# A two-block transformer kernel: the first up-projection of the second feed-forward scaled between the normed chunks, and products of zeros in the waits at the begin

## The chip, the cores and the metric

The kernel runs on one core of a Trainium2 chip. The metric is device time in microseconds: the median of several runs of the whole kernel, one launch each. TensorE is called PE here, VectorE DVE, ScalarE ACT, GpSimd POOL, and SyncE SP; SP issues most of the DMAs.

## The reference, cut to what matters

Two blocks of two layers each work on 256 tokens of width 1024 (first block: differential attention, then neighbourhood attention, each followed by a convolutional feed-forward, with a second stream of 256 context tokens; second block: two hybrid layers). The change touches the begin of the first layer and the feed-forward of the second layer:

```python
def rmsnorm(t, g):
    tf = t.astype(jnp.float32)
    tf = tf * lax.rsqrt(jnp.mean(tf * tf, axis=-1, keepdims=True) + NORM_EPS)
    return tf.astype(t.dtype) * g

def conv_ffn(t, w_up, w_conv, b_conv, w_down):
    n = t.shape[1]
    u = t @ w_up
    half = CONV_W // 2
    up = jnp.pad(u, ((0, 0), (half, half), (0, 0)))
    acc = b_conv
    for tap in range(CONV_W):
        acc = acc + up[:, tap:tap + n] * w_conv[tap]
    a, g = jnp.split(acc, 2, axis=-1)
    return (jax.nn.silu(g) * a) @ w_down
...
    for i in range(DEPTH):
        sh1, sc1, g1, sh2, sc2, g2 = jnp.split((silu_c @ ada_w[i] + ada_b[i])[:, None, :], 6, axis=-1)
        h = rmsnorm(x, norm_mix[i]) * (1.0 + sc1) + sh1
        ...
        x = x + g1 * y
        h2 = rmsnorm(x, norm_ffn[i]) * (1.0 + sc2) + sh2
        x = x + g2 * conv_ffn(h2, ffn_up[i], ffn_conv[i], ffn_conv_b[i], ffn_down[i])
```

## The kernel before

**Data and products.** Activations stand transposed, model dimension on the partitions: `xT` is 8 chunks (kc) of 128 rows by 512 columns, 256 tokens of x and 256 of the context. Every fp32 product is made of three products of shorter floats: an operand is split into a high and a low part, and `mm3` (L332, L335, L336) adds hi·hi, hi·lo and lo·hi in PSUM. `whi` and `wlo` are the parts of a weight tile: ACT copies `whi` from `raw` (L311), DVE subtracts to get `wlo` (L312). A normed chunk is made by three instructions: DVE's `nt` (L544: x times the column A times the token's factor `nbc`), ACT's `hhi` (L545), DVE's `hlo` (L546). A weight tile holds two units of 1024 columns, so it costs two L311 and two L312.

**Norms.** A norm sums squares (`naccx`, `naccc`), takes the mean over the partitions on PE (L512), computes the factor `nrstd` on POOL, spreads it over the partitions on PE (L532), and ACT copies it to `nbc` (L537). The modulation (`ada`) is a matrix-vector product: L384 on PE, ACT's copy `apart` (L393), L399 on PE, and three small DVE instructions that give the columns A and B.

**The begin.** `layer0` loads x, the first modulation piece and weights, calls `warm(14)`, which multiplies a tile of zeros by itself 14 times into an S bank, then makes the first norm, the modulation of chunk 0, the normed chunks 0 and 1 and their part of the V projection (L780). That stretch is in an order written by hand for PE, ACT and DVE; everything else is ordered by the Tile scheduler, which simulates the engines and lists each engine's instructions once. At run time each engine takes its list strictly in that order.

**PSUM.** Banks come from three pools: `acc` (2), `S` (3), `misc` (3). `acc5` takes acc and S in turn.

**The feed-forward.** Each up-projection j makes two tiles (`which` 0 and 1: the value and the gate) of 128 rows by 256 tokens over 8 chunks, 24 products each. Of the second layer's 22 up-projections, the first three are made before the norm is known, from x·A (`up_z`, `up_z_late`): their PSUM tiles (`pre[0]`, `pre[1]`, `pre[2]`; in `ffn` the list is `pre` and its pair of tiles `pz`) hold 256 unscaled columns and two columns of the shift. Once `nbc` is there, DVE copies the shift (L618, tag `nvar`, two buffers, the same tag as a small tile of `norm_rstd`), multiplies the tile by `nbc` into an `nt` buffer (L619), and ACT adds the shift (L620). After that come the convolution's three taps (ACT L625, DVE L628, POOL; for later up-projections DVE L628 and L637 read the PSUM tile itself), silu (L642) and the product on POOL.

**The chain.** `chain` (L719) plans two groups of norm steps that are set between the products of the late up-projections, 14 and 8 products apart: the mean, then the broadcast and the normed chunks. In the second layer all eight chunks are emitted there; then `up_z` of `pre[2]` goes out, and `ffn` begins, with the scalings of `pre[0]` first.

## Time and profile before

| | us |
|---|---|
| median of 3 runs | 1577.13 (1576.31 to 1577.66) |
| the profiled execution | 1575.77 |
| its span in the trace | 1574.0 |
| PE busy in the span | 1543.0 |
| DVE busy | 1118.6 |
| ACT busy | 770.7 |
| mean granted PE clock | 0.996 of full |

All rows below are of one execution. A window row gives the busy time of each engine and the granted clock of that stretch; a timeline row gives the start, the time from the first instruction's start to the last one's end, the instruction, its tiles and in brackets the idle time before it with what ended it. Consecutive instructions of a kind are one row, and neighbours overlap a little, so that start to start is a little shorter than one duration.

### The profile page before, as it was taken

To read this page: it belongs to the slowest core of one execution; us is meant where nothing else is said; L and a number is where in the kernel's file an instruction comes from. 1 tells how busy PE (TensorE), PEld (TensorE's weight loads), DVE (VectorE), ACT (ScalarE), POOL (GpSimd) and SP (SyncE) were. 2 spreads that over 40 slices of the span, in tenths; PEclk is the share of its full clock that TensorE was granted. 3 is DMA by queue.
4 is the path that set the end of the run, shared out by engine and by line. 5 is a ranking of instruction groups with operands and counts; after the bars stand their busy time and mean duration, and the time that the engine had idled before them with its cause. 6 is when DMAs were issued, how large, how long until landed. Compare 5 with 4: busy or idle time off the path is not lost.

```text
span 1574.0 us, 26745 instructions
## 1 busy us (share of the span) xinstructions
PE 1543.0 (98%) x10426; PEld 1352.5 (86%) x10426; DVE 1118.6 (71%) x2010; ACT 770.7 (49%) x1387; POOL 349.6 (22%) x419
## 2 busy tenths in 40 slices
PE   8999999999999999999999999999999999999998
PEld 6777777888888888888777999999899999989998
DVE  5456767787999999463554786777767667867665
ACT  4445544554422344343454574665655445555443
POOL 0012211321100111210112150124435123352222
PEclk9999999999999999999999999999999999999999
DMA  8523333134557554234221345547435556425552
GB/s 345 185 81 134 119 150 122 61 141 166 184 198 276 193 204 149 89 107 149 106 108 68 139 167 191 192 152 257 153 111 183 194 201 215 160 97 198 172 205 82
DMA packets 49373, 251.93 MB, mean 160 GB/s; under 512 B 5088, under 2 KB 8160, under 8 KB 31584
## 3 DMA queue, kind: packets, MB, share of 16 engines
q1 hardware_dynamic: 49248, 250.23, 44.3%
q8 instruction: 82, 1.34, 0.3%
q14 instruction: 43, 0.35, 0.1%
HBM read 249.16 MB, written 1.05 MB: 159 GB/s over the span
## 4 chain that ended last, share of the span: by engine, by line
PE 88%; DVE 5%; DMA 2%; ACT 2%; issue 1%; POOL 1%; SPq 0%; POOLq 0%; DVEq 0%; ACTq 0%
PE acc L332 13%; PE acc L336 13%; PE acc L335 12%; PE S L332 10%; PE S L336 10%; PE S L335 10%; PE S L1116 3%; PE S L780 2%; DMA raw<-in_aqk 1%; PE misc L1058 1%; PE misc L1165 1%; PE misc L1053 1%; PE misc L335 1%; PE misc L332 1%; PE misc L336 1%
## 5 line engine op out<-in xcount | busy, mean ns | idle before, releaser
L311 ACT ACTIVATE whi<-raw 128x1024 fp32r<-128x1024 f32 (+2 forms) x372 | 372.1, 1007 | 428.2 <-PE acc L335 167.9
L312 DVE TENSOR_TENSOR wlo<-raw,whi 128x1024 fp32r<-128x1024 f32 (+2 forms) x372 | 439.3, 1185 | 173.8 <-ACT whi L311 172.5
L332 PE MATMUL acc<-hhi,whi 128*128 128x256 f32 (+1 forms) x800 | 264.4, 331 | 2.0 <-DVE nt L619 1.4
L336 PE MATMUL acc<-hhi,wlo 128*128 128x256 f32 (+1 forms) x800 | 262.5, 329 | 0.3 <-DVE wlo L312 0.3
L335 PE MATMUL acc<-hlo,whi 128*128 128x256 f32 (+1 forms) x800 | 261.7, 327 | 0.1
L332 PE MATMUL S<-hhi,whi 128*128 128x256 f32 (+1 forms) x584 | 187.0, 320 | 1.8 <-DVE u L637 1.8
L336 PE MATMUL S<-hhi,wlo 128*128 128x256 f32 (+1 forms) x584 | 186.1, 319 | 0.0
L335 PE MATMUL S<-hlo,whi 128*128 128x256 f32 (+1 forms) x584 | 185.5, 318 | 0.0
L332 PEld LDWEIGHTS acc<-hhi,whi 128*128 128x128 f32 x800 | 150.3, 188 | 20.7 <-issue 6.3
L336 PEld LDWEIGHTS acc<-hhi,wlo 128*128 128x128 f32 x800 | 150.2, 188 | 17.7 <-issue 4.0
L335 PEld LDWEIGHTS acc<-hlo,whi 128*128 128x128 f32 x800 | 150.1, 188 | 16.4 <-issue 3.8
L441 DVE SCALAR_TENSOR_TENSOR junk<-araw,cb 128x1024 bf16<-128x1024 f32 x112 | 146.1, 1304 | 3.6 <-ACT cb L429 3.2
L643 POOL TENSOR_TENSOR u<-u,u 128x256 f32<-128x256 f32 (+1 forms) x46 | 58.2, 1266 | 371.7 <-ACT u L642 371.6
L332 PEld LDWEIGHTS S<-hhi,whi 128*128 128x128 f32 x584 | 111.4, 191 | 9.2 <-ACT ghi L361 2.0
L336 PEld LDWEIGHTS S<-hhi,wlo 128*128 128x128 f32 x584 | 111.1, 190 | 8.4
L335 PEld LDWEIGHTS S<-hlo,whi 128*128 128x128 f32 x584 | 111.1, 190 | 8.0
L1500 POOL TENSOR_TENSOR macc<-macc,mm 128x256 f32<-128x256 f32 x48 | 48.4, 1008 | 163.4 <-DVE mm L1498 163.4
L332 PE MATMUL acc<-hlo,whi 128*128 128x256 f32 x288 | 82.1, 285 | 0.0
L336 PE MATMUL acc<-hlo,wlo 128*128 128x256 f32 x288 | 81.5, 283 | 0.0
L335 PE MATMUL acc<-hhi,whi 128*128 128x256 f32 x288 | 81.4, 283 | 0.0
L332 PE MATMUL S<-ghi,whi 128*128 128x256 f32 (+1 forms) x209 | 68.6, 328 | 0.0
L336 PE MATMUL S<-ghi,wlo 128*128 128x256 f32 (+1 forms) x209 | 68.3, 327 | 0.0
(437 smaller groups left out, 3617.9 us busy)
## 6 DMA issues: line engine op xcount, KB each, us to landing
raw<-in_up SPq DMA_DIRECT2D x44, 1024.0 KB, 4.9
raw<-in_mg SPq DMA_DIRECT2D x32, 1024.0 KB, 5.2
araw<-in_adav SPq DMA_DIRECT2D x56, 512.0 KB, 4.2
raw<-in_t SPq DMA_DIRECT2D x24, 1024.0 KB, 4.8
raw<-in_down SPq DMA_DIRECT2D x32, 704.0 KB, 4.1
raw<-in_ada SPq DMA_DIRECT2D x16, 1024.0 KB, 4.9
raw<-in_aqk SPq DMA_DIRECT2D x8, 1024.0 KB, 5.9
raw<-in_bqk SPq DMA_DIRECT2D x8, 1024.0 KB, 4.9
```

Source lines behind the costliest of these rows:

```text
L311: nc.scalar.activation(hi[:, :n], raw, AF.Copy)
L312: nc.vector.tensor_tensor(lo[:, :n], raw, hi[:, :n].bitcast(F32), op=ALU.subtract)
L332: first = nc.tensor.matmul(ps, wh, x[0], start=start, stop=False)
L335: nc.tensor.matmul(ps, wh, x[1], start=False, stop=False)
L336: nc.tensor.matmul(ps, wl, x[0], start=False, stop=stop)
L441: nc.vector.scalar_tensor_tensor(junk, self.araw, 1.0, self.acb[0][:, c, :], op0=ALU.mult, op1=ALU.mult, accum_out=self.ada[l][:, v, k, c ...
L643: nc.gpsimd.tensor_tensor(us[0], us[0], us[1], op=ALU.mult)
L780: nc.tensor.matmul(ps, (hhi, hlo)[a][:, kc, c], w[b][:, f], start=(kc == 0 and e == 0), stop=(kc == KC - 1 and e == 2))
L1053: nc.tensor.transpose(tp[:, t * P : t * P + P], p[:, t * P : t * P + P], self.ident)
L1058: nc.tensor.matmul(o[64 * j : 64 * j + 64, :], v[:, t, (2 * h + j) * 64 : (2 * h + j) * 64 + 64], pT[:, j, t, :], start=(t == 0), stop=(t ...
L1116: m = self.nc.tensor.matmul(sps[j][:, :n], q[a][r, qs], k[b][r, ks], start=(e == 0), stop=(e == 2))
L1500: nc.gpsimd.tensor_tensor(acc, acc, m, op=ALU.add)
```

## The change

Three edits. The zero tile is made once and its products go to a `misc` bank instead of an S bank; there are 18 in front, and 2, 1 and 3 in three later places of the hand-written order. The scaling of an up-projection's tile moves into a helper `pz_scale`, and its shift gets a tag of its own, `pzs`. In the second layer, `chain` emits only chunks 0 to 3; then the two tiles of `pre[0]` are scaled, and then the chunks 4 to 7 are normed.

```diff
...
     def warm(self, n):
-        z = self.t(self.nrm, [P, T], "nbc", bufs=3)
-        self.nc.gpsimd.memset(z, 0.0)
-        ps = self.sb()
+        if self.zero is None:
+            self.zero = self.t(self.nrm, [P, T], "nbc", bufs=3)
+            self.nc.gpsimd.memset(self.zero, 0.0)
+        ps = self.misc()
         for _ in range(n):
-            self.nc.tensor.matmul(ps[:, 0:T], z[:, 0:P], z, start=True, stop=True)
+            self.nc.tensor.matmul(ps[:, 0:T], self.zero[:, 0:P], self.zero, start=True, stop=True)
+
+    zero = None
...
+    def pz_scale(self, pz, bc):
+
+        ps = self.t(self.nrm, [P, T], "nt", bufs=5)
+        shift = self.t(self.nrm, [P, 2], "pzs", bufs=2)
+        self.nc.vector.tensor_copy(shift, pz[:, T : T + 2])
+        self.nc.vector.tensor_tensor(ps, pz[:, 0:T], bc, op=ALU.mult)
+        return ps, shift
...
                         if pz:
-                            ps = self.t(self.nrm, [P, T], "nt", bufs=5)
-                            shift = self.t(self.nrm, [P, 2], "nvar", bufs=2)
-                            nc.vector.tensor_copy(shift, pz[which][:, T : T + 2])
-                            nc.vector.tensor_tensor(ps, pz[which][:, 0:T], bc, op=ALU.mult)
+                            ps, shift = pz[which] if isinstance(pz[which], tuple) else self.pz_scale(pz[which], bc)
                             nc.scalar.activation(ps, ps, AF.Identity, bias=shift[:, 0:1])
...
-    def chain(self, n, l, w, h, st, hh, done=None):
+    def chain(self, n, l, w, h, st, hh, done=None, kcs=range(KC)):
...
-            for kc in range(KC):
+            for kc in kcs:
...
-            self.warm(14)
+            self.warm(18)
...
                 rstd = self.norm_rstd(sts[0])
+                self.warm(2)
                 parts = self.ada_parts(0, ada[0])
+                self.warm(1)
                 bcs[0] = self.norm_bcast(rstd)
                 self.ada_columns(0, *parts)
+                self.warm(3)
...
-            self.chain((14, 8), 1, 1, 0, st2, (hhi, hlo), done)
+            self.chain((14, 8), 1, 1, 0, st2, (hhi, hlo), done, range(4))
             pre = self.up_z_late(1, range(2), 2)
             pre.append(self.up_z(1, 2, (self.misc, self.misc)))
             self.flush()
             bc = done[0]
+            pre[0] = pre[0][0], [self.pz_scale(ps, bc) for ps in pre[0][1]]
+            for kc in range(4, KC):
+                self.norm_half(1, 1, 0, kc, hhi, hlo, bc)
```

What this makes of the engines' lists is shown at three places. Rows read: line, operation, written tile, read tiles, and a count for equal rows; in the changed kernel the lines of `split`, `mm3` and the norm stand 3 lower down (L312 is L315, L544 is L547), those of `ffn` and `layer0` 8 lower down (L628 is L636, L780 is L788), and L605 and L606 of `pz_scale` do what L618 and L619 did. First PE at the kernel's begin, before (`nbc` is the tile of zeros in its first row, L512 the mean, L384 and L399 the modulation, L532 the broadcast, L780 the V projection):

```order
L303 MATMUL S_106<-nbc_104 128x256 x14
L512 MATMUL misc_143<-cst_69,p_132 128x2 x4
L384 MATMUL misc_152<-raw_95,cs_73 32x256 x8
L532 MATMUL misc_163<-cst_69,nrstd_150 128x128 x2
L399 MATMUL misc_152<-cst_69,apart_161 128x128 x2
L384 MATMUL misc_182<-ohi_88,cs_73 32x256 x8
L780 MATMUL acc_124<-whi_174,hhi_121 128x512
L780 MATMUL acc_125<-whi_174,hhi_121 128x512
```

And the same with the change:

```order
L304 MATMUL misc_106<-nbc_104 128x256 x18
L515 MATMUL misc_147<-cst_69,p_136 128x2 x4
L304 MATMUL misc_156<-nbc_104 128x256 x2
L387 MATMUL misc_159<-raw_95,cs_73 32x256 x8
L304 MATMUL misc_170<-nbc_104 128x256
L535 MATMUL misc_172<-cst_69,nrstd_154 128x128 x2
L402 MATMUL misc_159<-cst_69,apart_168 128x128 x2
L304 MATMUL misc_183<-nbc_104 128x256 x3
L387 MATMUL misc_195<-ohi_88,cs_73 32x256 x8
L788 MATMUL acc_128<-whi_187,hhi_125 128x512
L788 MATMUL acc_129<-whi_187,hhi_125 128x512
```

The zero products write misc tiles now and stand in four places, each ahead of a step that waits for another engine or a DMA.

Next ACT in the V projection of layer 0, where its last chunks are normed (`apart` is the modulation's copy); before:

```order
L311 ACTIVATE whi_103_543<-raw_98_511 128x1024
L311 ACTIVATE whi_114_595<-raw_113_593 128x1024
L393 ACTIVATE apart_95_493<-misc_94_484 128x256
L311 ACTIVATE whi_116_599<-raw_113_593 128x1024
L545 ACTIVATE hhi_18_121<-nt_101_517,ada0_6_76 128x256
L545 ACTIVATE hhi_18_121<-nt_102_533,ada0_6_76 128x256
L545 ACTIVATE hhi_18_121<-nt_105_547,ada0_6_76 128x256
L545 ACTIVATE hhi_18_121<-nt_106_563,ada0_6_76 128x256
```

With the change:

```order
L314 ACTIVATE whi_106_556<-raw_101_524 128x1024
L314 ACTIVATE whi_117_608<-raw_116_606 128x1024
L548 ACTIVATE hhi_18_125<-nt_104_530,ada0_6_76 128x256
L396 ACTIVATE apart_98_506<-misc_97_497 128x256
L548 ACTIVATE hhi_18_125<-nt_105_546,ada0_6_76 128x256
L314 ACTIVATE whi_119_612<-raw_116_606 128x1024
L548 ACTIVATE hhi_18_125<-nt_108_560,ada0_6_76 128x256
L548 ACTIVATE hhi_18_125<-nt_109_576,ada0_6_76 128x256
```

Two of the four hhi that stood behind the second whi of that weight tile (`whi_116`, now `whi_119`) now stand ahead of it, one of them ahead of `apart` too.

Last DVE ahead of the second layer's feed-forward, before (`acc_1455` and `S_1456` are the two tiles of `pre[0]`; `nt_1473` to `nt_1476` are the chunks 4 to 7, and the last of the L546 in a row is chunk 4's):

```order
L312 TENSOR_TENSOR wlo_1514_8169<-raw_1510_8162,whi_1513_8168 128x1024
L546 SCALAR_TENSOR_TENSOR hlo_1449_7853<-nt_1470_7960,ada1_7_77,hhi_1448_7852 128x256
L546 SCALAR_TENSOR_TENSOR hlo_1449_7853<-nt_1471_7964,ada1_7_77,hhi_1448_7852 128x256
L546 SCALAR_TENSOR_TENSOR hlo_1449_7853<-nt_1472_7968,ada1_7_77,hhi_1448_7852 128x256
L546 SCALAR_TENSOR_TENSOR hlo_1449_7853<-nt_1473_7972,ada1_7_77,hhi_1448_7852 128x256
L544 SCALAR_TENSOR_TENSOR nt_1474_7976<-xT_3_71,nA11_11_81,nbc_1468_7954 128x256
L312 TENSOR_TENSOR wlo_1521_8237<-raw_1519_8234,whi_1520_8236 128x1024
L544 SCALAR_TENSOR_TENSOR nt_1475_7980<-xT_3_71,nA11_11_81,nbc_1468_7954 128x256
L544 SCALAR_TENSOR_TENSOR nt_1476_7984<-xT_3_71,nA11_11_81,nbc_1468_7954 128x256
L619 TENSOR_TENSOR nt_1486_8084<-acc_1455_7864,nbc_1468_7954 128x256
L312 TENSOR_TENSOR wlo_1523_8241<-raw_1519_8234,whi_1522_8240 128x1024
L619 TENSOR_TENSOR nt_1490_8095<-S_1456_7865,nbc_1468_7954 128x256
```

With the change, from the first of chunk 0 to 3 on (the tiles of `pre[0]` are `acc_1458` and `S_1459`):

```order
L547 SCALAR_TENSOR_TENSOR nt_1472_7969<-xT_3_71,nA11_11_81,nbc_1471_7967 128x256
L547 SCALAR_TENSOR_TENSOR nt_1473_7973<-xT_3_71,nA11_11_81,nbc_1471_7967 128x256
L547 SCALAR_TENSOR_TENSOR nt_1474_7977<-xT_3_71,nA11_11_81,nbc_1471_7967 128x256
L547 SCALAR_TENSOR_TENSOR nt_1475_7981<-xT_3_71,nA11_11_81,nbc_1471_7967 128x256
L606 TENSOR_TENSOR nt_1483_8075<-acc_1458_7877,nbc_1471_7967 128x256
L605 COPY pzs_1486_8080<-S_1459_7878 128x2
L315 TENSOR_TENSOR wlo_1480_8022<-raw_1476_8015,whi_1479_8021 128x1024
L315 TENSOR_TENSOR wlo_1515_8178<-raw_1513_8175,whi_1514_8177 128x1024
```

and a little later in the same list (`nt_1487` to `nt_1489` are the chunks 4 to 6):

```order
L606 TENSOR_TENSOR nt_1485_8079<-S_1459_7878,nbc_1471_7967 128x256
L315 TENSOR_TENSOR wlo_1524_8250<-raw_1522_8247,whi_1523_8249 128x1024
L547 SCALAR_TENSOR_TENSOR nt_1487_8083<-xT_3_71,nA11_11_81,nbc_1471_7967 128x256
L547 SCALAR_TENSOR_TENSOR nt_1488_8087<-xT_3_71,nA11_11_81,nbc_1471_7967 128x256
L547 SCALAR_TENSOR_TENSOR nt_1489_8091<-xT_3_71,nA11_11_81,nbc_1471_7967 128x256
L315 TENSOR_TENSOR wlo_1526_8254<-raw_1522_8247,whi_1525_8253 128x1024
L636 SCALAR_TENSOR_TENSOR u0_1493_8106<-nt_1483_8075,vec_4_72,u0_1493_8106 128x255
L605 COPY pzs_1502_8135<-S_1466_7926 128x2
L636 SCALAR_TENSOR_TENSOR u1_1495_8113<-nt_1485_8079,vec_4_72,u1_1495_8113 128x255
L549 SCALAR_TENSOR_TENSOR hlo_1452_7866<-nt_1487_8083,ada1_7_77,hhi_1451_7865 128x256
L549 SCALAR_TENSOR_TENSOR hlo_1452_7866<-nt_1488_8087,ada1_7_77,hhi_1451_7865 128x256
L549 SCALAR_TENSOR_TENSOR hlo_1452_7866<-nt_1489_8091,ada1_7_77,hhi_1451_7865 128x256
```

The readout of the acc tile moved from behind all eight L544 to behind the fourth, that of the S tile ahead of the last four; chunks 4 to 7 and their hlo stand behind it, the hlo also behind the first tap of both tiles.

## Rows read from the trace of the kernel before

**Rows 1.** The page: busy time by engine, and the chain that ended last

```profile
PE 1543.0 (98%) x10426; PEld 1352.5 (86%) x10426; DVE 1118.6 (71%) x2010; ACT 770.7 (49%) x1387; POOL 349.6 (22%) x419
...
PE 88%; DVE 5%; DMA 2%; ACT 2%; issue 1%; POOL 1%; SPq 0%; POOLq 0%; DVEq 0%; ACTq 0%
```

**Rows 2.** Windows: length, busy time (count) by engine, granted clock, DMA share, GB/s

```profile
300.00:325.00 25.00, 21.17 (x169) 21.00 (x168) 23.12 (x50) 15.25 (x34) 9.98 (x11) 0.93 0.23 85
...
900.00:925.00 25.00, 21.73 (x174) 21.37 (x174) 22.64 (x42) 20.85 (x38) 13.07 (x17) 0.94 0.46 171
```

**Rows 3.** Timeline of PE at the begin: start, length, instruction, [idle before, releaser]

```profile
1.08 9.35 PE L303 MATMUL S<-nbc 128*128 128x256 f32 x28 [1.08 <-POOL nbc L300]
...
7.67 2.54 PE L303 MATMUL S<-nbc 128*128 128x256 f32 x11
...
10.96 1.05 PE L512 MATMUL misc<-cst,p 128*128 128x2 f32 x8 [0.54 <-DVE p L493]
12.13 1.07 PE L384 MATMUL misc<-raw,cs 128*32 128x256 f32 x16
...
15.87 1.07 PE L384 MATMUL misc<-ohi,cs 128*32 128x256 f32 x16 [1.74 <-DMA ohi<-in_ada]
```

**Rows 4.** Timeline of PE and ACT in the V projection of layer 0

```profile
27.85 0.50 PE L780 MATMUL S<-whi,hhi 128*128 128x512 f32 x1 [0.54 <-ACT hhi L545]
...
56.97 1.06 ACT L311 ACTIVATE whi<-raw 128x1024 fp32r<-128x1024 f32 x1 [1.20 <-PE misc L780]
...
58.48 0.73 PE L780 MATMUL acc<-whi,hhi 128*128 128x512 f32 x2 [1.32 <-ACT hhi L545]
```

**Rows 5.** Timeline of PE and ACT at the first feed-forward's begin

```profile
322.11 0.99 PE L512 MATMUL misc<-cst,naccc 128*128 128x2 f32 x4 [3.83 <-DVE naccc L481]
...
329.10 0.57 ACT L625 ACTIVATE u<-S,vec 128x256 f32<-128x256 f32 x1 [2.64 <-PE S L336]
```

**Rows 6.** Timeline of PE at the second feed-forward's begin

```profile
904.01 0.28 PE L335 MATMUL S<-hlo,whi 128*128 128x256 f32 x1
...
907.46 0.36 PE L332 MATMUL acc<-hhi,whi 128*128 128x256 f32 x1 [1.43 <-DVE nt L619]
907.65 0.28 PE L335 MATMUL acc<-hlo,whi 128*128 128x256 f32 x1
...
908.90 0.28 PE L332 MATMUL acc<-hhi,whi 128*128 128x256 f32 x1
...
921.33 0.35 PE L332 MATMUL S<-hhi,whi 128*128 128x256 f32 x1 [1.84 <-DVE u L637]
...
922.38 0.42 PE L335 MATMUL S<-hlo,whi 128*128 128x256 f32 x1
922.59 0.42 PE L336 MATMUL S<-hhi,wlo 128*128 128x256 f32 x1
```

**Rows 7.** Windows of 3 us there, columns as in rows 2

```profile
921.00:924.00 3.00, 2.67 (x15) 2.70 (x16) 3.00 (x6) 2.97 (x6) 3.00 (x4) 0.67 0.52 218
924.00:927.00 3.00, 3.00 (x22) 3.00 (x21) 2.45 (x5) 1.74 (x4) 2.90 (x3) 0.76 0.72 284
```

**Rows 8.** Timeline of DVE in the same stretch

```profile
897.13 2.06 DVE L544 SCALAR_TENSOR_TENSOR nt<-xT,nA,nbc 128x256 f32<-128x256 f32 x5
...
899.18 2.35 DVE L312 TENSOR_TENSOR wlo<-raw,whi 128x1024 fp32r<-128x1024 f32 x2
...
902.98 1.68 DVE L546 SCALAR_TENSOR_TENSOR hlo<-nt,ada,hhi 128x256 fp32r<-128x256 f32 x4
...
906.88 0.43 DVE L619 TENSOR_TENSOR nt<-acc,nbc 128x256 f32<-128x256 f32 x1
...
920.71 0.47 DVE L637 SCALAR_TENSOR_TENSOR u<-S,vec,u 128x255 f32<-128x255 f32 x1
```

**Rows 9.** Timeline of ACT in the same stretch

```profile
913.15 1.05 ACT L311 ACTIVATE whi<-raw 128x1024 fp32r<-128x1024 f32 x1
...
914.61 1.28 ACT L642 ACT_TABLE_LOAD   x1
```

## The prediction

> **What bounds the kernel now.** I read the page's busy times and chain first. TensorE (PE) is busy 1543.0 of the span's 1574.0 us, and the chain that ended last is 88% PE [rows 1]: what the change can win or lose is idle PE time, and PE time at the lower clock. So I went to the windows of 25 us and looked for stretches where PE is busy for less than the window or the granted clock is under 1.00. Two that the change reaches are 300 to 325 us (21.17 busy, clock 0.93) and 900 to 925 us (21.73 busy, clock 0.94) [rows 2]. The third place is the begin, read on PE's timeline: zero products to 10.43 us, a wait of 0.54 us, and one of 1.74 us for a DMA ahead of the second L384 [rows 3]. Everywhere else PE is close to full, and the change moves nothing there.
>
> **The begin: ten zero products more.** The 14 old ones leave two records each, 28 in all; late ones take 2.54 us for 11 records, so 0.23 us a record and, since neighbours overlap a little, about 0.43 us a product [rows 3]. The change sets 18 ahead of the first L512 and 2, 1 and 3 behind it.
> - Four more in front: 4 x 0.43 = 1.72 us, so they end at 10.43 + 1.72 = 12.15. L512 could start at 10.96 and now starts at 12.15: +1.19. The rest is in its idle 0.54.
> - The later groups: 2 x 0.43 = 0.86 and 1 x 0.43 before the nrstd and apart products. The first L384, at 12.13, moves to 12.13 + 1.19 + 0.86 = 14.18; PE's old work ended at 14.13 (15.87 less the idle 1.74) and ends at 14.13 + 1.19 + 0.86 + 0.43 = 16.61.
> - Three more: 1.29, to 17.90. The second L384 started at 15.87, when its DMA had landed. It is late by 17.90 − 15.87 = 2.03 us, and so is the first L780 behind it. Of ten products (4.30 us) 2.27 lie in waits and **2.03** on the path.
> What is late next: the L780 of the first eight chunks. Some of it comes back near 58 us, where PE waited 1.32 us for ACT's hhi, which stood behind the weight copy whi at 56.97 (1.06 us), itself kept 1.20 us by PE's L780 into misc [rows 4]. In ACT's new order one of the two hhi of that place stands ahead of whi and of apart, and needs only an nt that VectorE (DVE) has made by then. I count the 1.32 as given back: 2.03 − 1.32 = **+0.7**. Bounds: none of it comes back, +2.0; the 0.54 at 27.85 [rows 4] also absorbs, 2.03 − 1.32 − 0.54 = +0.2. A gain below nothing is possible only by the clock: if an execution loses a stretch at half clock after the pause at 14.13, as this one did after a pause of 1.84 near 920 (below), zeros in the pause save up to 1.6, which puts the lower end at −1.4. In this trace nothing was lost there, so I take +0.7.
>
> **The first feed-forward (around 320 us).** Only the tag of the shifts changes there, with what the scheduler makes of it. PE waits 3.83 us at 322.11 for naccc, a chain that the change doesn't touch, and ACT's L625 at 329.10 waits 2.64 us for PE [rows 5]. Copies that move earlier by some tenths, and a table load that moves into that idle time of ACT, are hidden by these two waits. I take 0; the bounds are one half-clock stretch more or less, ±1.6.
>
> **The second feed-forward (895 to 930 us).** Here lies the case. Two waits of PE: 1.43 us at 907.46 for an acc bank, which DVE's L619 at 906.88 reads out, and 1.84 us at 921.33 for an S bank that DVE's L637 at 920.71 frees [rows 6, 8]. Together 3.27, just the 25 − 21.73 of the window [rows 2]. [...]
> - What the change moves: L619 on pre 0's acc stood behind all eight L544; now it stands behind four. On DVE: from 897.13, four L544 at 2.06/5 = 0.41 end at 898.77, the readout takes 0.43, so the bank is free at about 899.2 instead of 907.2 [rows 8]. PE's wait of 1.43 goes, since PE comes to it at 906.0 (907.46 less 1.43).
> - What comes late instead: the chunks 4 to 7. Going on from 899.2 with the durations of [rows 8] and the new order: copy 0.1, two wlo 2.35, hlo 0.42, wlo 1.18, three hlo 1.26, copy 0.1, the S readout 0.43, wlo 1.18, three L544 1.23, wlo 1.18, then L628 0.47, a copy, L628 0.47, and hlo of chunk 4 0.42: 910.1. Rows overlap by some 5%, so 909.2 to 910.1; I take 909.7. Before, that hlo was the fourth of the four that start at 902.98. PE now has the chunks 0 to 3 of three up-projections to do meanwhile, 36 products of 0.114 from 904.0 on [rows 6] and the last of pre 2's that move in among them, to 908.5, and hi·hi products of chunk 4 up to 908.8. New wait: **0.9** (0.4 to 1.7).
> - ACT: the whi at 913.15 stood behind the first of pre 2's scalings [rows 9]. Now the table load of 1.28 us and all of pre 1's and most of pre 2's work stand ahead of it; it ends about 915.9, its wlo at 917.1, and PE wants that at about 916.2. New wait: 0.5 to 1.0, and I take **1.0**.
> - The S bank: pre 0's elementwise work starts earlier on ACT, and the L625 and L637 that free the bank come earlier by the same, about 919.6; PE comes there at 919.9. The wait of 1.84 goes.
> - Clock: waits of 1.43 and 1.74 us in this trace were not followed by the lower level, 1.84 and 3.83 were [rows 3, 5, 6, 7]. The two new waits are about 1 us, so I count the 1.7 as saved.
> Sum: −3.27 + 0.9 + 1.0 − 1.7 = **−3.1**. Bounds: −5.0 with no new wait, and +2.4 with both at their worst (rival 4).
>
> [...]
>
> **The sum.** On the profiled execution (1575.77 us, the span of 1574.0 and 1.8 around it): +0.7 + 0 − 3.1 = −2.4, so 1573.4. That execution is 1.36 below the median of the three runs, 1577.13, and the prediction is for a median: 1577.13 − 2.4 = **1574.7**.
>
> **Rivals.**
> 1. No new waits, and the zeros hidden: hlo of chunk 4 comes in time because DVE's wlo needn't wait for ACT as I assumed. −5.0 + 0.2 = −4.8: 1572.3. For it: my replay is at the early end with the overlaps. Against: eleven instructions now stand ahead of that hlo.
> 2. The clock doesn't follow the wait. The lower level would fall somewhere near 922 whatever PE waited for; or one of the new waits brings it. +0.7 − 3.27 + 1.9 = −0.7: 1576.4. For it: 1.74 without and 1.84 with a drop are close together. [...]
> 3. The change does not do what it says: banks come free earlier, yet PE waits as long for chunk 4 (1.6) and the next weights (1.7), and the clock falls all the same. Only the zeros remain, +0.7: 1577.8.
> 4. **Slower.** Chunk 4's activations become the bound. One mechanism: on DVE and ACT the scalings of pre 0 are ahead of chunks 4 to 7. If hlo of chunk 4 comes at 910.1 and PE at 908.4, the wait is 1.7, and with one more table load of 1.28 [rows 9] on ACT the wlo wait is 1.0 + 1.3 = 2.3: 4.0 in place of 3.27. Both are then as long as the wait that brought the lower clock: 2 x 1.7 in place of 1.7. That is +0.7 + 1.7 = +2.4, and with the zeros' 2.03 not given back +4.4: 1581.5. It decides from where the wait for hlo is as long as the one at 921.33.
>
> **How the numbers follow.** A measurement of this kernel can tell about 0.2% (3.2 us) from no change: faster means under 1574.0, slower over 1580.3. Chances: forecast 0.40 (its own spread about ±1.5, so 0.12 of it under 1574.0), rival 1 0.24, rival 2 0.16, rival 3 0.10, rival 4 0.10 (0.08 over the bound). Faster 0.12 + 0.24 = 0.36, slower 0.08, the same 0.56. The range goes from half a us under rival 1 to just over rival 3, 1571.8 to 1578.6; most of rival 4 and the lower tail of rival 1 stay outside, about 0.2.
>
> **What would show it.** In the profile after: PE's wait for the S bank from L637 and that for the acc bank from the readout gone; granted clock 1.00 through 920 to 930 (else rival 2); a wait for hlo of chunk 4 near 909 and one for wlo near 917, each about 1 us (none: rival 1; as long as the old 1.84: rival 4); the second L384 at about 17.9, and no wait of 1.3 near 58. It is wrong as a whole if the window of 320 us moves by over 2 us, since I gave it nothing, or if PE's idle time shows up at a place where the orders are the same.

## The result and the profile after

The changed kernel takes 1586.84 us (median of 4 runs, 1585.66 to 1587.42) against 1576.82 of the kernel before: 1.0061 times as long, interval 1.0049 to 1.0074. It is ten us slower, where 2.4 less was forecast and 1578.6 was the range's upper end. Its page, busy times by engine:

```profile
span 1585.1 us, 26784 instructions
...
PE 1559.5 (98%) x10446; PEld 1363.4 (86%) x10446; DVE 1122.1 (71%) x2010; ACT 770.8 (49%) x1387; POOL 353.1 (22%) x419
```

Set beside [rows 1] this says that the loss is not idle time. PE's idle time fell from 1574.0 − 1543.0 = 31.0 us to 1585.1 − 1559.5 = 25.6. But PE's busy time rose by 16.5 us, and ten zero products account for 4.3 of that, by the prediction's 0.43 each. The waits of PE (what it waited for: us in total, times, longest), 850 to 960 us of the changed kernel:

```profile
PE S L338 <- DVE hlo L549: 1.3, 1, 1.3
PE S L339 <- DVE wlo L315: 1.2, 2, 0.8
PE acc L335 <- ACT ohi L364: 0.5, 1, 0.5
PE acc L335 <- ACT whi L314: 0.4, 1, 0.4
```

The two waits of [rows 6] are gone, and the two that I had foreseen are there, for hlo of chunk 4 and for wlo. The windows that answer [rows 2] (length, busy time and count by engine, granted clock, DMA share, GB/s) and the begin that answers [rows 3]:

```profile
300.00:325.00 25.00, 21.18 (x176) 20.99 (x175) 22.87 (x49) 15.52 (x36) 9.38 (x11) 0.98 0.24 85
900.00:925.00 25.00, 22.96 (x189) 22.44 (x189) 21.49 (x41) 19.23 (x33) 11.21 (x13) 1.00 0.36 127
925.00:950.00 25.00, 25.00 (x213) 25.00 (x212) 24.93 (x39) 19.92 (x36) 11.92 (x11) 1.00 0.51 185
```

```profile
1.08 10.79 PE L304 MATMUL misc<-nbc 128*128 128x256 f32 x36 [1.08 <-POOL nbc L301]
...
13.56 1.07 PE L387 MATMUL misc<-raw,cs 128*32 128x256 f32 x16
...
17.15 1.07 PE L387 MATMUL misc<-ohi,cs 128*32 128x256 f32 x16
18.15 0.73 PE L788 MATMUL acc<-whi,hhi 128*128 128x512 f32 x2
```

The stretch at 900 us runs at full clock and is idle for 2.0 us instead of 3.3; the second L384 (now L387) starts at 17.15 without a wait. So the time went where no engine is waited for. To find it I took landmarks on PE's timeline, the first products of the means (L512), and made segments of them:

| us between landmarks | before | after | difference |
|---|---|---|---|
| start to 322.11 (layer 0) | 322.11 | 322.96 | +0.9 |
| 322.11 to 679.78 (first feed-forward, 512-column products) | 357.67 | 362.17 | +4.5 |
| 679.78 to 891.01 (layer 1's attention) | 211.23 | 212.30 | +1.1 |
| 891.01 to 1084.41 (second feed-forward) | 193.40 | 192.69 | −0.7 |
| 1084.41 to 1566.63 (hybrid layers) | 482.22 | 487.73 | +5.5 |

Most of the loss is in the first feed-forward and the hybrid layers, whose code and order the change hardly touches. Windows in the middle of long streams of products show why. Before, then after (PE is busy throughout at clock 1.00; the count in the first brackets is its products, about two more than start in the window):

```profile
500.00:600.00 100.00, 100.00 (x439) 82.05 (x438) 98.86 (x147) 40.01 (x51) 12.84 (x8) 1.00 0.59 206
960.00:1060.00 100.00, 100.00 (x851) 100.00 (x850) 72.85 (x110) 57.93 (x93) 11.65 (x13) 1.00 0.52 183
```

```profile
500.00:600.00 100.00, 100.00 (x432) 81.10 (x431) 97.90 (x143) 37.84 (x48) 11.51 (x7) 1.00 0.57 201
960.00:1060.00 100.00, 100.00 (x845) 100.00 (x845) 71.30 (x107) 55.15 (x87) 11.38 (x12) 1.00 0.52 181
```

From the start of one product to the start of the next (the spacing, from here on) a product of 512 columns takes 100/437 = 0.229 us before and 100/430 = 0.2325 after, one of 256 columns 117.8 ns and 118.7. In these windows PE never waits, its clock is full, and it still takes its products 0.8 to 1.5% more slowly. The products of the hybrid layers that read ahi lose more, 113.4 ns before and 119.9 after (means of 382 spacings each), over 5%. Before, then after, ahead of the last mean:

```profile
1545.00:1562.00 17.00, 17.00 (x152) 17.00 (x152) 11.35 (x19) 6.62 (x11) 8.05 (x6) 1.00 0.04 13
```

```profile
1556.00:1573.00 17.00, 17.00 (x144) 17.00 (x144) 10.33 (x18) 6.61 (x11) 7.34 (x6) 1.00 0.00 1
```

### The profile page after: what moved, and what is told of

It reads as the page before. It is cut to its first block, busy times and chain, and to the rows that moved or that the text cites. A ratio compares the mean times of both kernels' runs of the same rounds, so it can differ in the third digit from the quotient of the medians.

```text
span 1585.1 us, 26784 instructions
## 1 busy us (share of the span) xinstructions
PE 1559.5 (98%) x10446; PEld 1363.4 (86%) x10446; DVE 1122.1 (71%) x2010; ACT 770.8 (49%) x1387; POOL 353.1 (22%) x419
## 3 DMA queue, kind: packets, MB, share of 16 engines
q8 instruction: 82, 1.34, 0.3%
## 4 chain that ended last, share of the span: by engine, by line
PE 91%; DVE 4%; ACT 2%; DMA 1%; issue 1%; POOL 1%; POOLq 0%; DVEq 0%; ACTq 0%
PE acc L335 13%; PE acc L339 13%; PE acc L338 13%; PE S L335 10%; PE S L339 10%; PE S L338 10%; PE S L1130 3%; PE S L788 2%; DMA raw<-in_aqk 1%; PE misc L387 1%; PE misc L1072 1%; PE misc L1067 1%; PE misc L335 1%; PE misc L339 1%; PE misc L338 1%
## 5 line engine op out<-in xcount | busy, mean ns | idle before, releaser
L315 DVE TENSOR_TENSOR wlo<-raw,whi 128x1024 fp32r<-128x1024 f32 (+2 forms) x372 | 438.5, 1183 | 166.3 <-ACT whi L314 165.3
L338 PE MATMUL S<-glo,whi 128*128 128x256 f32 (+1 forms) x209 | 68.8, 329 | 0.0
```

The source lines that it names most:

```text
L315: nc.vector.tensor_tensor(lo[:, :n], raw, hi[:, :n].bitcast(F32), op=ALU.subtract)
L338: nc.tensor.matmul(ps, wh, x[1], start=False, stop=False)
```

## What sets the spacing: places in memory

The one thing that the change does everywhere is to move tiles. The new tag `pzs` takes 64 bytes of the norm pool, and all tiles behind it (hhi, hlo, ghi, glo, v, ahi, alo and the rest) stand 64 bytes further up in SBUF: hhi starts at byte 112640 instead of 112576, while the weight buffers `whi` and `wlo` stay (64128 the first). Theory A says that this decides, theory B that the order, the zeros or the PSUM banks do. The first four runs keep one apart from the other.

**e1**: the change without the move; the shift borrows the buffers of a small tile that is used only later.

```diff
-        shift = self.t(self.nrm, [P, 2], "pzs", bufs=2)
+        shift = self.t(self.nrm, [P, 2], "nr2", bufs=2)
```

> The changed kernel, but the shift tile pzs takes the buffers of the small tile nr2 (used only at the end of the first block), so that every SBUF tile stands where it stood before the change. Theory A (the 64 bytes of pzs push hhi, hlo, ghi and all that lies behind them up, and TensorE takes its products more slowly from there): the steady spacing of the 512-column products is back at 229 ns (232 with the change) and the time is 1573 to 1577. Theory B (the new order, the zero products or the PSUM banks that they turn do it): 1585 to 1588, spacing 232.

Measured: 1568.06 us, ratio 0.9951 (0.9937 to 0.9966). **e2**: the move without the change, the instructions of the kernel before one for one.

```diff
-        r2 = self.t(self.nrm, [P, 2], "nr3", bufs=2)
+        r2 = self.t(self.nrm, [P, 16], "nr3", bufs=2)[:, 0:2]
```

> The kernel before, instruction for instruction, with one small tile of the norm pool 64 bytes larger in all, so that hhi, hlo, ghi and all behind them stand 64 bytes further up, as with the change. Theory A: spacing of 512-column products 232 ns, of 256-column products 118.7 instead of 117.8, time 1585 to 1592 (the change's 1586.8 without what its order saves). Theory B: 1576 to 1578, spacing 229.

Measured: 1592.44, ratio 1.0100 (1.0085 to 1.0115). **e3** and **e4**: the move by 32 bytes (`bufs=3` for nr3) and by −64 (`bufs=1` for nr2 and nr3).

> The kernel before with the same tiles 32 bytes further up, half way. Theory A in the form that only the start within a block of 64 bytes or more matters: a start off the 64-byte grid is as slow as or slower than the 64 of the change, 1585 or more. Theory A in the form of a distance between tiles: anything from 1570 to 1590. Theory B: 1576 to 1578.

> The kernel before with the same tiles 64 bytes further down. Theory A with a special bad place at a multiple of 1024 bytes (where the change puts hhi): about 1577, as before. Theory A where every place has its own spacing: another time than 1577, to either side by up to 12. Theory B: 1576 to 1578.

Measured: 1596.26 (1.0130, 1.0106 to 1.0154) and 1587.86 (1.0068, 1.0052 to 1.0083). Windows as above, e1, then e2, then e3, then e4:

```profile
500.00:600.00 100.00, 100.00 (x439) 82.05 (x438) 98.89 (x147) 40.05 (x52) 13.45 (x8) 1.00 0.59 202
960.00:1060.00 100.00, 100.00 (x851) 100.00 (x851) 74.42 (x110) 58.57 (x96) 13.66 (x15) 1.00 0.55 189
```

```profile
500.00:600.00 100.00, 100.00 (x432) 81.08 (x431) 97.65 (x143) 38.07 (x48) 11.53 (x7) 1.00 0.61 211
960.00:1060.00 100.00, 100.00 (x845) 100.00 (x845) 72.19 (x109) 55.92 (x88) 10.96 (x12) 1.00 0.52 182
```

```profile
500.00:600.00 100.00, 100.00 (x430) 80.43 (x430) 97.35 (x144) 38.89 (x49) 11.43 (x7) 1.00 0.59 202
960.00:1060.00 100.00, 100.00 (x835) 100.00 (x835) 71.41 (x108) 55.98 (x88) 10.96 (x12) 1.00 0.51 181
```

```profile
500.00:600.00 100.00, 100.00 (x443) 82.81 (x442) 99.90 (x144) 39.66 (x50) 10.29 (x7) 1.00 0.59 202
960.00:1060.00 100.00, 100.00 (x835) 100.00 (x835) 70.00 (x106) 54.95 (x86) 10.77 (x12) 1.00 0.51 179
```

e1 has the counts of the kernel before and e2 those of the change. e2's page has about the change's busy time, with the instructions of the kernel before and no product added:

```profile
PE 1559.8 (98%) x10426; PEld 1363.6 (86%) x10426; DVE 1119.5 (70%) x2010; ACT 770.5 (48%) x1387; POOL 349.0 (22%) x419
```

Theory B falls: e1 keeps all that it names and is not slow, e2 has none of it and is. e3 and e4 show that neither a grid of 64 bytes nor one bad place explains it: 64 bytes down, 512-column products get faster (443: 226.8 ns) and 256-column products slower (835: 120.0).

**Which place counts?** e5 moves the weight buffers and the activations up together; e6 only the weights.

```diff
-  ... self.t(self.per, [P, KC, 2], f"nA{l}{w}") ...
+  ... self.t(self.per, [P, KC + 8 * l * w, 2], f"nA{l}{w}")[:, 0:KC] ...
```

(64 bytes ahead of the weights; e6 also has `bufs=1` for nr2 and nr3, which takes 64 off behind them.)

> The kernel before, instruction for instruction, with the weight buffers (raw, whi, wlo), the norm pool, hhi, hlo and everything behind them 64 bytes further up: the activations stand as in the run with only the activations up, but the distance between weights and activations is as before. If the distance between the two operands decides: 1575 to 1579, spacing 229 and 117.8 ns. If the activations' own place decides: 1590 to 1594, spacing 232.3 and 118.7. Anything else: the weights' own place counts too.

> The kernel before, instruction for instruction, with the weight buffers and the norm pool 64 bytes further up, and hhi, hlo and all behind them where they were: the distance is that of the run with the activations 64 down. If the distance decides: 1585 to 1589, spacing 226.7 and 120.0 ns. If the activations' own place decides: 1575 to 1579, spacing 229 and 117.8. Anything else: the weights' own place counts too.

Measured: e5 1576.21, ratio 0.9999 (0.9990 to 1.0009); e6 1585.11, ratio 1.0054 (1.0039 to 1.0069). e6's windows:

```profile
500.00:600.00 100.00, 100.00 (x443) 82.81 (x442) 99.90 (x144) 39.41 (x50) 10.47 (x7) 1.00 0.58 201
960.00:1060.00 100.00, 100.00 (x836) 100.00 (x835) 72.07 (x109) 57.57 (x92) 11.66 (x13) 1.00 0.53 184
```

These are the counts of e4, at the activations' old address. So it is the **distance** between the weight tile that is loaded and the activations that stream. The other engines write and read both places too, and the traces speak against them as the cause. From 930 to 1040 us of the change, the products that pass while ACT is idle stand 118.6 ns apart and those that pass while it is busy 118.7; for DVE it is 118.6 and 118.7, and without a DMA packet under way 118.7. In the kernel before it is 117.8 in each of these cases, and in e4 all 917 spacings there are 120 ns. That leaves PE, which reads both tiles: the distance of the pair changes the kernel's time by up to 1.3% (e3). How PE comes to depend on it was not shown.

**How far does the rule reach?** Four kernels place tiles by it, all with the changed order, the changed zeros and e1's borrowed buffers: e10 to e12 put hhi and hlo ahead of the norm pool, with a pad of 0, 64 and 128 bytes; e9 moves the norm pool ahead of the weight buffers and pads, so that hhi, hlo, ghi, glo, ahi and alo all stand at 192 beyond a multiple of 512.

```diff
         self.st = ctx.enter_context(self.pool("stream"))
+        self.pad = ctx.enter_context(self.pool("pad"))
+        self.t(self.pad, [P, 16], "pad")
+        self.hpool = ctx.enter_context(self.pool("hh"))
         self.nrm = ctx.enter_context(self.pool("nrm"))
```

(e11; e10 has no pad, e12 32 columns.) e9:

```diff
-        self.st = ctx.enter_context(self.pool("stream"))
         self.nrm = ctx.enter_context(self.pool("nrm"))
+        self.st = ctx.enter_context(self.pool("stream"))
+        self.pad = ctx.enter_context(self.pool("pad"))
+        self.t(self.pad, [P, 48], "pad")
...
+        t(hp, [P, 32], "ahpad")
         ahi = t(hp, [P, KC, T], "ahi", F32R)
```

> The changed kernel with the weight buffers moved so that the distance from a weight tile to hhi, hlo, ghi, glo and ahi, alo is 192 bytes beyond a multiple of 512 (320 for hhi and ghi, 192 for ahi in the kernel before). In the kernel before, the products from ahi (1300 and 1550 us) stand 113.3 to 114 ns apart and in all runs with another distance there 118.7 to 119.6. Theory (the distance modulo 512 sets the spacing): the 256-column products stand at 113.3 everywhere, about 4.4 ns less for some 4500 of them, so 20 us less than the changed kernel at old places: 1545 to 1556, more if the 512-column products are slower than 229. Rival (the fast stretches are a state that other work brings): 1566 to 1572.

> The changed kernel with hhi and hlo ahead of the norm pool: distance of hhi 0 modulo 512, of ghi (320) and ahi (192) as in the kernel before. If the distance modulo 512 decides: products from ghi (second feed-forward's down-projections) 117.8 ns and from ahi 113.3 to 114 as before, those from hhi another spacing between 113 and 121, one that stays the same in all phases that read hhi. If nothing but the order of pools counts: 1587 to 1592 as with every other move.

> As the run before this one, 64 bytes further: hhi 64, ghi 384, ahi 256. Products from ghi at 118.7 and from ahi at 119.5, as in the changed kernel; those from hhi another spacing, open. Time by that 1570 to 1600.

> Once more 64 bytes further: hhi 128, ghi 448, ahi 320. Products from ahi at 117.8 (the spacing of 320), from hhi at the spacing that ahi had at 128, 118.9; from ghi open. Time 1575 to 1600.

Measured: 1575.81 (1.0003, 0.9986 to 1.0020), 1576.91 (1.0004, 0.9992 to 1.0015), 1577.63 (1.0007, 0.9993 to 1.0020), 1582.11 (1.0032, 1.0020 to 1.0043). e9's two windows, the first of e10, and both of e12:

```profile
500.00:600.00 100.00, 100.00 (x430) 80.70 (x429) 97.54 (x142) 38.79 (x49) 11.48 (x7) 1.00 0.59 200
960.00:1060.00 100.00, 100.00 (x885) 100.00 (x884) 74.64 (x113) 59.73 (x96) 12.82 (x14) 1.00 0.55 191
```

```profile
500.00:600.00 100.00, 100.00 (x443) 82.80 (x442) 99.82 (x148) 41.06 (x53) 14.02 (x8) 1.00 0.61 205
```

```profile
500.00:600.00 100.00, 100.00 (x432) 81.07 (x432) 97.88 (x143) 37.84 (x48) 11.51 (x7) 1.00 0.58 201
960.00:1060.00 100.00, 100.00 (x859) 100.00 (x858) 72.14 (x109) 56.79 (x89) 11.37 (x12) 1.00 0.54 185
```

Put in order, the distances tried repeat after 256 bytes, by the count of the window from 500 us: hhi at 0 modulo 512 (e10: 443) spaces like hhi at 256 (e4, e6: 443), 64 (e11: 438) like 320 (before: 439), 128 (e12: 432) like 384 (the change: 432). In e10 to e12 hhi and ghi (the activations of the down-projections) stand at different distances in one execution, and each has the spacing of its own: in e12's window from 960 us, with 859 products, those that read hhi (128) stand 118.7 ns apart and those that read ghi (448, so 192) 113.4. The table gives the mean spacing of consecutive products of one kind of tile in the traces, 350 to 600 us and 960 to 1060 (ghi within 0.1 of the value given):

| distance modulo 256 | tiles | 512 columns, ns | 256 columns, ns |
|---|---|---|---|
| 0 | hhi in e4, e6, e10 | 226.7 | 120.0 |
| 64 | hhi in before, e1, e5, e11; ghi in e10 | 228.9 | 117.8 |
| 96 | hhi in e3 | 233.3 | 120.0 |
| 128 | hhi in the change, e2, e12; ghi in e11 | 232.4 | 118.7 |
| 192 | hhi in e9; ghi in e12 | 233.3 | 113.3, in other phases 117.8 |

My expectation of e9 was right on the mechanism in the second feed-forward (885: 113.3 ns) and wrong on the sum: its 512-column products are as slow as any here, and its hybrid layers stay at 117.8, though ahi at the same distance gave 113.3 in the kernel before. At 192, 256 columns had two spacings. It is so at 64 as well: between its two waits the kernel before has the products of hhi at 113.3 ns [rows 6], and from 925 us at 117.8:

```profile
908.00:918.00 10.00, 10.00 (x91) 10.00 (x90) 7.64 (x19) 8.70 (x15) 7.92 (x11) 1.00 0.29 107
930.00:940.00 10.00, 10.00 (x87) 10.00 (x86) 9.24 (x17) 6.05 (x12) 2.49 (x2) 1.00 0.41 156
```

The last runs look into that.

## The order and the zeros, with the distance put back

**e7** is the order of the second feed-forward alone (14 zeros as before), **e8** the zeros alone, **e13** the whole change with pzs in its own buffers and the weights 64 bytes further up, all at the old distance.

```diff
e7, beside e1's edit
-            self.warm(18)
+            self.warm(14)
...
-                self.warm(2)
...
-                self.warm(1)
...
-                self.warm(3)
```

(with the `warm` of the kernel before). e8 is the kernel before with the lines of the change that touch `warm`. e13 is the change with

```diff
-  ... self.t(self.per, [P, KC, 2], f"nA{l}{w}") ...
+  ... self.t(self.per, [P, KC + 8 * l * w, 2], f"nA{l}{w}")[:, 0:KC] ...
...
-        t = self.t(self.nrm, [P, 2], "nr2", bufs=2)
+        t = self.t(self.nrm, [P, 2], "nr2", bufs=1)
...
-        r2 = self.t(self.nrm, [P, 2], "nr3", bufs=2)
+        r2 = self.t(self.nrm, [P, 2], "nr3", bufs=1)
```

> The changed order of the second feed-forward alone: 14 zero products as before, pzs in nr2's buffers, so all tiles at their old places. Theory: the order gives the 2.3 us that the profile of the run at old places shows between 890 and 950 us, and the begin (2.5 us by 102 us there) is the zero products': 1574 to 1575.5. Rival: the gain at the begin is the order's too (the hhi ahead of a weight copy near 57 us comes with it): 1571 to 1573.

> The kernel before with the zero products of the change alone (18, 2, 1, 3, into a misc bank), all tiles at their old places. Theory: 2.5 us less by 102 us, and in some executions more where the old kernel loses a stretch at half clock after its pause near 14 us: 1572 to 1575. Rival (my prediction): 2.0 late, with up to 1.3 given back: 1577 to 1579. Granted clock between 10 and 30 us 1.00.

> The changed kernel with pzs in its own buffers, and the weight buffers 64 bytes further up, so that all distances are those of the kernel before at other addresses. If the distance alone made the change slow: the time of the run at old places, 1566 to 1572, against 1586.8 for the change as given. If the borrowed buffer or the addresses made that run fast: 1574 to 1587.

Measured: e7 1575.58, ratio 0.9993 (0.9983 to 1.0002); e8 1574.77, 0.9992 (0.9982 to 1.0002); e13 1572.53, 0.9966 (0.9952 to 0.9981). e13 confirms e1 at other addresses: without the move, the change is a gain of some 5 to 8 us (e1's interval, −9.9 to −5.4 us, and e13's, −7.6 to −3.0, overlap). At the change's own distance it is the same: 1586.84 against 1592.44 in e2. e7 and e8 apart are each about 1 us and within 0.2%; their sum falls short of e13, and the segments show that single executions differ by more than the parts are worth:

| us between landmarks | before | e5 | e7 | e8 | e1 | e13 |
|---|---|---|---|---|---|---|
| start to 322.11 | 322.11 | 323.64 | 326.29 | 320.07 | 318.94 | 321.56 |
| 322.11 to 679.78 | 357.67 | 357.06 | 357.85 | 359.32 | 358.23 | 358.29 |
| 891.01 to 1084.41 | 193.40 | 193.39 | 191.49 | 191.38 | 191.49 | 191.49 |

The new order takes 193.4 − 191.5 = 1.9 off the second feed-forward, in each profile of this table that has it. So does e8, without it: the zeros' misc banks made the scheduler list some of this phase's work in another order too (its lists for PE, DVE and ACT differ from before near here), and its waits there are 1.4 for the acc bank and three for wlo, 1.3 in all, with no 1.8. Both parts reach the same 191.4, so their gains in this phase don't add. In this table the begin with the new zeros takes 318.9 to 321.6, with the old ones 322.1 to 326.3. The clock tells part of it. Windows of e7 (old zeros), then of e1 (new zeros), 11 to 16 us:

```profile
11.00:16.00 5.00, 4.53 (x37) 2.81 (x40) 0.64 (x4) 1.43 (x3) 0.70 (x1) 0.66 1.01 415
```

```profile
11.00:16.00 5.00, 5.00 (x41) 3.73 (x40) 0.92 (x5) 1.61 (x3) 0.70 (x1) 1.00 1.01 402
```

With the old zeros five of seven profiles have the lower clock there (e5 and e7 0.66, e2 and e3 0.64, e4 0.54); e6 and the execution of before that I had read have not. With the new zeros the twelve profiles here and the change's own are at 1.00 in these 5 us, though eight of the thirteen (the change's among them, 0.72 from 25 to 30 us) have a stretch at the lower clock near 27, as three of the seven have with the old ones. The stretch from 11 to 16 us is not behind the pause at 14.13, where the prediction looked for it: in e5 the clock is 0.50 from 12 us on, behind a wait of 1.10 us ahead of L512, and the later pause is 0.20. In e6 the waits at these places are 1.34 and 2.06, and the clock stays at 1.00. e5, then e6:

```profile
10.37 1.05 PE L512 MATMUL misc<-cst,p 128*128 128x2 f32 x8 [1.10 <-DVE p L493]
...
15.44 1.07 PE L384 MATMUL misc<-ohi,cs 128*32 128x256 f32 x16 [0.20 <-DMA ohi<-in_ada]
...
12.00:15.00 3.00, 3.00 (x22) 1.71 (x14) 0.00 (x0) 0.53 (x2) 0.40 (x1) 0.50 0.99 413
```

```profile
10.13 1.05 PE L512 MATMUL misc<-cst,p 128*128 128x2 f32 x8 [1.34 <-DVE p L493]
...
15.41 1.07 PE L384 MATMUL misc<-ohi,cs 128*32 128x256 f32 x16 [2.06 <-DMA ohi<-in_ada]
...
12.00:15.00 3.00, 1.35 (x14) 0.72 (x6) 1.36 (x5) 2.05 (x4) 0.16 (x1) 1.00 0.98 408
```

And for the second feed-forward, e5 (old order, old distance), then e7 (new order):

```profile
900.00:925.00 25.00, 21.73 (x178) 21.37 (x177) 22.65 (x42) 21.27 (x38) 12.62 (x17) 0.96 0.47 171
925.00:950.00 25.00, 25.00 (x208) 25.00 (x208) 22.19 (x37) 17.15 (x32) 7.76 (x8) 0.97 0.47 170
```

```profile
900.00:925.00 25.00, 22.84 (x189) 22.27 (x188) 23.74 (x44) 20.54 (x37) 13.55 (x14) 1.00 0.34 127
925.00:950.00 25.00, 25.00 (x214) 25.00 (x214) 24.84 (x40) 19.12 (x34) 10.38 (x10) 1.00 0.58 203
```

The drop after the wait of 1.8 us is there in both profiles of the old order at the old distance (0.94 from 900 to 925 us in the kernel before [rows 2], 0.96 in e5); in e2, e3, e4 and e6, where the wait is 1.2 (PE's products are slower there, so it should come to that bank later, an estimate), there is none (1.00 from 900 to 950 us), and none in the thirteen profiles with the new order.

**e14** and **e15** use the distances: e14 reads hhi and hlo of the second feed-forward 32 columns further on in the same tiles and pads ghi, so that only this phase has 192 modulo 256; e15 also puts the 512-column phases at 0 (hlo at 64). Both have e1's borrowed buffers; e14's edit:

```diff
-            hhi, hlo = self.new_h()
+            hhi, hlo = [z[:, :, 32:288] for z in self.new_h()]
...
         with self.pool(f"ffn{l}") as fp:
+            if l:
+                self.t(fp, [P, 32], "fpad")
```

> The changed kernel at old places; only hhi, hlo (by reading other columns of the same tiles) and ghi, glo of the second feed-forward stand 128 bytes further from the weights: 192 modulo 256 in place of 64. If the distance sets the spacing by phase: equal to the run at old places up to 895 us, then 113.3 ns in place of 117.8 for some 1300 products between 940 and 1080 us, 5 to 6 us less: 1561 to 1566. If the spacing there is a state that comes with what ran before: no change, 1566 to 1572.

> The changed kernel with a distance for each phase, modulo 256: hhi 0 (hlo 64) and ghi 0 where products have 512 columns, 192 in the second feed-forward, 64 and 192 in the hybrid layers as in the kernel before. If distances add up by phase: 226.7 to 229 ns up to 650 us (2 to 3 us less than at old places), 113.3 in the second feed-forward (5 to 6 less), the rest as before: 1558 to 1564. If other waits take the place in the 512-column phases, as the run with the activations 64 down hinted: 1562 to 1567.

Measured: 1572.29 (0.9971, 0.9960 to 0.9983) and 1570.05 (0.9973, 0.9961 to 0.9986): no better than e1 and e13. e15's part on the 512 columns failed: its window from 500 us counts 433 products (232 ns) and not the 443 of distance 0, as slow as at 128. It failed where hhi stands at 0 and hlo at 64, which together are no mean of the two; the products that read ghi, with both parts at 0, have 226.7. The single times fall into two groups, e14's at 1567.4 to 1568.1 and 1571.2 to 1574.2, e15's at 1568.5 to 1570.3 and 1574.6 to 1576.4. e14's first profile is of the lower group and has 113.3 ns in the second feed-forward, e15's is of the upper group and has 117.8. **e16**, **e17** and **e18** are second profiles of e15, e14 and e1.

> The same kernel as e15, one more profile. Theory (the spacing of a phase is a state that an execution falls into): 1568 to 1570.5 with 113.3 ns between 960 and 1060 us, or 1574 to 1577 with 117.8; the two go together. Rival (the groups come from the clock's stretches alone): 117.8 at either time, or a time between the groups.

> The same kernel as e14, one more profile. Its first fell at 1568.1 with 113.3 ns. Theory: 1571 to 1574 with 117.8, or 1567 to 1569 with 113.3. Rival (the distance of 192 gives 113.3 every time): 113.3 at any time.

> The same kernel as e1, one more profile. Its first fell at 1570.8 with 117.8 ns. Theory: 1570 to 1574 with 117.8, or 1565 to 1568.5 with 113.3 in one phase (960 to 1060 us or another). Rival: 117.8 at any time.

Measured: e16 1569.43, e17 1571.96, e18 1572.87. The window from 960 us of e15, then of e16, then of e14, then of e17:

```profile
960.00:1060.00 100.00, 100.00 (x852) 100.00 (x851) 73.15 (x110) 57.94 (x94) 11.69 (x13) 1.00 0.54 185
```

```profile
960.00:1060.00 100.00, 100.00 (x885) 100.00 (x884) 77.11 (x115) 61.22 (x100) 13.62 (x15) 1.00 0.57 196
```

```profile
960.00:1060.00 100.00, 100.00 (x885) 100.00 (x884) 76.64 (x114) 61.29 (x100) 15.09 (x17) 1.00 0.57 194
```

```profile
960.00:1060.00 100.00, 100.00 (x852) 100.00 (x851) 74.32 (x110) 58.54 (x97) 13.64 (x15) 1.00 0.54 188
```

With the same kernel and the same clock there are 852 products in one execution and 885 in the next, and the time goes with it: 1576.4 and 1569.4 for e15, 1568.1 and 1572.0 for e14. So at a distance of 192 this phase had one of two spacings, 117.8 or 113.3 ns, and an execution fell into one of them. The traces of e15 and e16 show where it changed: at a short gap in PE's stream. In e15 the products from 922.8 to 925.2 us stand 113.4 ns apart, then come spacings of 158 and 194 ns at the step from an S tile to an acc tile, and from 925.6 on they stand 117.8 apart. In e16 they stand 117.9 apart up to the same step, which has one spacing of 156, and 113.3 behind it. What decides the outcome of such a gap is not shown. At 64, e1's and e13's groups (1566 to 1568 and 1571 to 1575) look the same, but no profile caught the lower one: e1 and e18 have 851. That those groups have this cause is not shown.

## Why the prediction was wrong, step by step

- **The sum has no term for where tiles stand.** The step that failed is the one that confined the change to three places, "Everywhere else PE is close to full, and the change moves nothing there.", and with it the one on the tag: "Only the tag of the shifts changes there, with what the scheduler makes of it." I asked what the new tag does to the order and not what it does to the addresses behind it, and put its cost at nothing. It costs 1586.84 − 1572.53 = 14.3 us (e13; 18.8 by e1), or 1592.44 − 1576.9 = 15.5 without the change (e2). None of the rivals had it; the "slower" rival was another mechanism, with waits that did not come. The text's own test, "if PE's idle time shows up at a place where the orders are the same", looked at the wrong quantity: it was PE's busy time.
- **The second feed-forward, −3.1 forecast.** Measured −1.9 (e1, e7, e13). The two old waits went and the clock stayed up, as forecast. The wait for hlo is 1.4 instead of 0.9 (e1). wlo has two waits, 1.2 in all; e5, with the old order, has one of 0.4, so 0.8 is new where 1.0 was forecast. A spacing makes up another 0.5: the old order ran 907 to 919 us at 0.114 [rows 6], the new one at 117.8 ns, over some 100 products. Counted with the sum's 1.7 for the clock, about 0.4 is not located. The mechanism was right and the size was two thirds.
- **The clock there.** In this phase my reading, that the drop follows the longer wait, fits the runs: it comes with 1.8 us and not with 1.2 or 1.4. At the begin it does not: a wait of 1.10 in e5 comes with a drop, and waits of 1.34 and 2.06 in e6 with none. So the length of the wait alone does not decide, and rival 2 is not excluded as a reading of the clock; the drop was gone all the same, in each profile of the new order. No run shows the sum's 1.7 as such. What the kernel before shows behind the wait is a granted clock of 0.67 and 0.76 over two windows of 3 us [rows 7], 3 × 0.33 + 3 × 0.24 = 1.7 us short of full, and 17 spacings that take 3.54 us (921.99 to 925.53 us) where 17 at 117.8 ns take 2.00, so 1.5 us lost; what the changed kernel, e1 and e7 show there is 1.00 from 900 to 950 us.
- **The begin, +0.7 forecast.** The path came out as worked out (the second L384 at 17.15 after, 17.90 forecast; no wait near 58 us), but the sign was wrong: with the old distance the first 322 us are shorter by 0.6 to 3.2 (e1, e13) than in the profile of before, and by more against e5 (323.6) and e7 (326.3). I had seen the possibility, zeros that save a half-clock stretch, and put it at the end of the range because the one execution that I had read has none. Five of seven with the old zeros have one, e5 with the same instructions among them, though from 12 us on and not behind the pause at 14.13, where I had looked for it. Apart from that, e8 alone does not clear 0.2%, so the size of this term stays uncertain.
- **The first feed-forward's begin, 0 forecast.** At the old distance 322 to 680 takes 358.2 to 358.3 (e1, e13) against 357.1 and 357.7 (e5, before): about half a us to one longer, inside the ±1.6. That 1.6 for a stretch at half clock is an estimate; [rows 2] show 25 × (1 − 0.94) = 1.5 us short of full in the window at 900 us.
- **Without the move** the forecast of 1574.7 would have come near: e13's 1572.5 lies within its range and e1's 1568.1 below it. That nearness is in part luck, since the begin's sign was wrong and the second feed-forward's gain too large. The total was wrong by a term that no wait in the profile could show.

## What to carry to other kernels

When a change adds, drops or resizes a buffer, compare the addresses of all tiles behind it before costing anything else, and keep them where they were (here, by borrowing a buffer that is free at that time), so that a timing compares the change and not the move. When busy time of PE grows and its waits do not, divide a long full window by its count of products, before and after: the spacing is the first suspect. One profile is one execution: here the begin, whose stretches at the lower clock come and go, and the spacing of a phase each differed by several us between executions.

## What the runs showed of the hardware

- The spacing of back-to-back fp32 products (weights of 128 columns loaded for each) went with the distance between weight tile and streamed operand, and was the same at 0 and 256, 64 and 320, 128 and 384 bytes (modulo 512): over the five distances tried modulo 256, 226.7 to 233.3 ns for 512 columns and 113.3 to 120.0 for 256. What was best for one width was not for the other: 0 was the fastest for 512 columns and, with 96, the slowest for 256. In the change it was the same whether ACT, DVE or the DMAs were at work or not (118.6 to 118.7 ns). Why is open; no run looked inside PE.
- At a distance of 192 the second feed-forward ran at 113.3 or 117.8 ns, and which of the two differed from one execution of a kernel to the next (e14 and e17, e15 and e16). From the mean at 319 to 322 us to the one at 1076 to 1085 us the slower execution took 5.5 (e15 over e16) and 6.0 us longer (e17 over e14). In e15 and e16 the spacing changed at a short gap in PE's stream (156 to 194 ns at 925.4 us). What decides which is open.
- A stretch at half clock from about 12 us came in some executions of the same instructions and not in others (before: none, 1.00 from 12 to 15 us; e5: 0.50 from 12 to 15 us, mean 0.66 from 11 to 16). It came behind a wait of 1.10 us (e5) and did not come with waits of 1.34 and 2.06 (e6: 1.00 from 12 to 15 us).
